# Reading the moving operand of a matmul alternately from two stretches: dense, block and value products of a two-layer hybrid encoder

## The chip, the cores and the metric

The kernel runs on one core of one Trainium2 chip. The metric is the device time of one execution in microseconds (us). Three runs of the kernel before the change took 1018.16, 1019.00 and 1019.24 us, a median of 1019.0 us. The profile shown here was taken from one further execution.

## The reference

The encoder has two layers on 512 tokens of 1024 features, in float32. Layer 0 mixes tokens with stick-breaking attention (16 heads of 64), layer 1 with a gated linear recurrence (RG-LRU); each is followed by an MLP with a squared ReLU. Cut to what matters:

```python
for layer in range(2):
    h = rms_norm(x, norm_mix[layer])
    if layer == 0:
        q, k, v = split(h @ w_qkv)               # 1024 -> 3 x 1024
        y = stick_breaking(q, k, v) @ w_o        # 1024 -> 1024
    else:
        proj = h @ w_in                          # 1024 -> 2 x 1024: gate, and input of the recurrence
        xc = causal_conv4(proj[:, 1024:])
        r, i = sigmoid(blocks(xc, w_a) + b_a), sigmoid(blocks(xc, w_x) + b_x)   # 16 blocks of 64 x 64
        y = (scan(r, i, xc) * gelu(proj[:, :1024])) @ w_ro
    x = x + y
    h = rms_norm(x, norm_mlp[layer])
    x = x + square(relu(h @ w1)) @ w2            # 1024 -> 4096 -> 1024
return rms_norm(x, norm_final)
```

## The kernel before

Activations lie with features on the 128 partitions and the 512 tokens along the free dimension (`x[c]`, c = 0..7). Every float32 product is made of three products of `float32r` halves: each operand is split into a high half (ScalarE, a `CAST`) and a low half (VectorE, a subtraction), and the matmuls high x high, low x high and high x low add up in one PSUM bank. So each of these products costs PE three matmuls, ACT one cast and DVE one subtraction of the weights (`wh`, `wl`).

There are four kinds of large products, named by the line of their matmul:

- **Dense**, L244 to L246 (`three`, called by `dense`, `beside` and the step generators): a 128x128 piece of a weight is stationary, and 512 tokens of one feature chunk (`xgh`, `xgl`, or `bh`, `bl`) stream past it. Query, key, attention output, the first quarter of each up-projection (`squared`), both halves of `w_in`, the output projection `w_ro`. L452 does the same for the first query and key; L1591 to L1593 for the gates of the recurrence.
- **Value**, L506 to L508 (`v_steps`): 128 tokens are stationary, and 256 columns of the value weight stream.
- **Block**, L1024 (`Mlp.up`): the other three quarters of the up-projection are done by a fast scheme with seven block products in place of eight; 256 tokens stream past a piece of 128 weight columns.
- **Down**, L1123 (`Mlp.times`): the down-projection in the same scheme. Activations are stationary, and 512 weight columns stream. These weights are stored on the host so that the program can read them alternately: the access pattern takes element 0 of the first 256 columns, then element 0 of the second 256, then element 1 of the first, and so on (`rearrange("p j (i n) -> p j n i", i=2)`), and the results land in PSUM in natural order. All other products read their moving operand straight through.

Scores (L590, L591) and the products of attention weights with values (L657, L658) are further matmuls, and L631 and L1406 are transposes on PE.

The order of the work on PE is the order in which the code calls it. Attention interleaves the fill (dense and value steps) with chains of scores and values by a table of due times (`SCORE0`, `VAL0`, `PACE`, in fill steps). The recurrence goes by the hand-written list `ORDER`, in which `P` is a dense product, `n` multiplies its PSUM bank by the norm factor (`scaled`), `b` and `t` are the convolution taps (`first_tap` on ACT, `taps` on DVE), `G` and `s` the gates and their sigmoids, and `z` the gate branch. In the MLP each step's weights are split some four steps ahead (`prepare`, `make`). On the other engines the steps of the recurrence and the MLP stand in the order of the code as well. There are eight PSUM banks, so a bank that is read late holds up the product that wants it next.

Consumers that read a PSUM bank of these products: `parted` and `k_halves` (query and key), `so_part`, `residual` (x plus product), `squared`, `leave` (the block products), `scaled`, `sigmoids`, `gate`.

Of the kernel before, what the change touches and what calls it, by code (L numbers as in the profile page):

```python
# [18 lines left out]
P = 128  # L19
# [48 lines left out]
def hybrid_encoder(  # L68
# [40 lines left out]
    def f(ap):  # L109
        return ap.bitcast(F32)  # L110

# [130 lines left out]
    def three(ps, ah, al, wh, wl, start, stop):  # L242

        PE.matmul(ps, wh, ah, start=start, stop=False)  # L244
        PE.matmul(ps, wl, ah, start=False, stop=False)  # L245
        PE.matmul(ps, wh, al, start=False, stop=stop)  # L246
# [68 lines left out]
    with ExitStack() as actx:  # L315
# [39 lines left out]
        def parted(x, tag):  # L355
# [3 lines left out]
            A.copy(xh, x)  # L359
            V.tensor_tensor(xl, x, f(xh), ALU.subtract)  # L360
            return xh, xl

        def q_halves(pair, ps):
            q[pair] = stacked("q", parted(ps, "x"))

        def first_halves(pq, pk):

            qh, ql = parted(pq, "x")
            h = hp.tile([P, S], F32R, tag="th", name="th", bufs=3)
            l = hp.tile([P, S], F32R, tag="tl", name="tl", bufs=3)  # L370
            A.copy(h, pk)
            V.tensor_tensor(l, pk, f(h), ALU.subtract)
# [9 lines left out]
        def k_halves(pair, ps):  # L382
            ks = hp.tile([P, S], F32, tag="ks", name="ks", bufs=1)
            V.tensor_tensor(ks, ps, norm["r"], ALU.mult)
            h, l = parted(ks, "x")
# [35 lines left out]
        with tc.manual_schedule(engines=others):  # L421
# [64 lines left out]
        def v_steps(m, tags=("acc",) * NB):  # L486
# [14 lines left out]
            for t in range(NB):  # L501
                ts = slice(t * P, (t + 1) * P)
                ps = bank(tags[t])[:, : 2 * P]
                for k in range(C):
                    wh, wl = (u[:, k % 4, :] for u in ws[k // 4])
                    PE.matmul(ps, xgh[:, k, ts], wh, start=k == 0, stop=False)  # L506
                    PE.matmul(ps, xgh[:, k, ts], wl, start=False, stop=False)
                    PE.matmul(ps, xgl[:, k, ts], wh, start=False, stop=k == C - 1)  # L508
# [12 lines left out]
        def so_part(c):  # L521
# [3 lines left out]
            for k in range(EARLY):  # L525
                three(ps, bh[:, k, :], bl[:, k, :], wh[:, k, :], wl[:, k, :], k == 0, k == EARLY - 1)
                if k == EARLY - 1:
                    early[c] = hp.tile([P, S], F32, tag="early", name="early")
                    A.copy(early[c], ps)
# [230 lines left out]
    def add_x(c, ps):  # L760
        V.tensor_tensor(x[c], x[c], ps, ALU.add)

    def residual(srcs, gname, begun={}, ready={}):

        for c in range(C):
            add_x(c, begun[c][0] if c in begun else dense(srcs[c], bh, bl, halves=ready.get(c)))
# [29 lines left out]
    class Mlp:  # L796
# [64 lines left out]
        def squared(self, c, also=None):  # L861
# [13 lines left out]
            self.A.activation(t, ps.rearrange("p (h n) -> p h n", h=2), AF.Relu)  # L875
# [139 lines left out]
        def up(self, name, w, ps, new):  # L1015
# [3 lines left out]
            for i in range(2):  # L1019
                for k in range(C // 2):  # L1020
                    h, l = self.xa(block, k)
                    wh, wl = (t[:, k, i * P : (i + 1) * P] for t in w)
                    for n, (m, y) in enumerate(((wh, h), (wl, h), (wh, l))):
                        PE.matmul(  # L1024
                            ps[:, i * HS : (i + 1) * HS], m, y,
# [134 lines left out]
        def run(self, first, between, end):  # L1160
# [89 lines left out]
            def leave(i):  # L1250
# [28 lines left out]
                u, three = us[p], bank.rearrange("p (i n) -> p i n", i=2)  # L1279
                keep = {"P1": 0, "P6": 1, "P5": 2, "P7": 3}.get(name)  # L1280
                if keep is not None:

                    self.A.copy(u[keep], three)
                at, x, y, op = {
                    "P3": (1, three, u[1], ALU.subtract),
                    "P7": (2, u[2], u[3], ALU.subtract),
                    "P2": (0, u[0], three, ALU.add),
                    "P4": (3, three, None, None),
                }.get(name, (None,) * 4)
                if op:  # L1290
                    self.V.tensor_tensor(u[at], x, y, op)
# [589 lines left out]
```

## Time and profile before

| | |
|---|---|
| median of three runs | 1019.0 us |
| the profiled execution | 1019.2 us |
| its span, first to last instruction | 1017.3 us |
| granted TensorE clock | 0.999 |
| idle time of ACT before its casts `wh<-b`, in all | 99.7 us |
| HBM read over the span | 139.51 MB |

A row of a timeline gives start, length, engine, line, operation, what it writes and reads, and the shape. Matmuls are pipelined: the length of one overlaps the next, so what a matmul costs PE is the distance from its start to the next one's start. A row of a stretch gives its length, and then per engine the busy time with the number of instructions in brackets.

### The profile page before, as it was taken

The numbers are of one execution on the slowest core, as the hardware profiler recorded it, in microseconds if no ns is written. First come the engines' busy times: TensorE is split into PE (matmuls) and PEld (weight loads), VectorE is DVE, ScalarE is ACT, GpSimd is POOL, SyncE is SP. The second block draws the span as 40 slices with busy tenths as digits, with TensorE's granted clock in tenths as the row PEclk, the third lists the DMA queues.
The fourth block names the chain that finished last, engine by engine and source line by source line (L and its number), as shares of the span: only waits on it lengthen the run. The fifth ranks groups of instructions, "written<-read, shape, count | busy, mean of one in ns | idle before, by whom it ended". The sixth has DMA issues, their size and how long they took to land.

```text
span 1017.3 us, 15902 instructions
## 1 busy us (share of the span) xinstructions
PE 1004.5 (99%) x5836; PEld 889.2 (87%) x5836; DVE 858.3 (84%) x1152; ACT 714.6 (70%) x1110; POOL 180.0 (18%) x243
## 2 busy tenths in 40 slices
PE   9999999999999999999999999999999999999997
PEld 7888888878888988998988888888889989989985
DVE  6878787857898799799799789985887799898898
ACT  6777676745778775774776699973887774874865
POOL 0454444430000110111011210300011110111112
PEclk9999999999999999999999999999999999999999
DMA  7845344536638667667783464445448977977953
GB/s 236 222 125 146 104 144 105 167 104 228 188 84 212 151 165 205 166 154 199 167 236 85 133 180 123 124 172 201 103 85 209 205 164 193 227 163 199 218 117 106
DMA packets 71901, 165.71 MB, mean 163 GB/s; under 512 B 23824, under 2 KB 25104, under 8 KB 71824
## 3 DMA queue, kind: packets, MB, share of 16 engines
q1 hardware_dynamic: 59424, 123.54, 38.4%
q0 software_dynamic: 11680, 40.38, 23.7%
q8 instruction: 46, 0.75, 0.3%
q10 hardware_dynamic: 720, 0.79, 0.2%
q14 instruction: 31, 0.25, 0.1%
HBM read 139.51 MB, written 6.29 MB: 143 GB/s over the span
## 4 chain that ended last, share of the span: by engine, by line
PE 65%; DVE 15%; ACT 11%; issue 5%; DMA 2%; POOL 0%; DVEq 0%; SPq 0%; ACTq 0%; POOLq 0%
PE ps_t L1123 9%; PE ps_acc L244 5%; PE ps_acc L246 5%; PE ps_acc L245 5%; PE ps_acc L1123 5%; PE ps_acc L1024 5%; ACT wh L786 4%; DVE wl L786 4%; DVE u L786 3%; ACT u L786 3%; PE ps_z L1123 3%; PE ps_t L244 2%; PE ps_t L245 2%; PE ps_t L246 2%; DVE b L786 2%
## 5 line engine op out<-in xcount | busy, mean ns | idle before, releaser
L786 ACT CAST wh<-b 128x1024 fp32r<-128x1024 f32 x168 | 173.8, 1047 | 99.7 <-DVE b L786 49.8
L786 DVE TENSOR_TENSOR wl<-b,wh 128x1024 fp32r<-128x1024 f32 x168 | 203.7, 1221 | 40.5 <-ACT wh L786 39.6
L1101 POOL DMA_DIRECT2D b<-in_w_dn x40 | 35.0, 876 | 347.7 <-DVE b L786 155.6
L244 PE MATMUL ps_acc<-xg,wh 128*128 128x512 f32 x200 | 81.7, 409 | 0.0
L1024 PE MATMUL ps_z<-xg,wh 128*128 128x256 f32 x384 | 78.9, 277 | 0.0
L246 PE MATMUL ps_acc<-xg,wh 128*128 128x512 f32 x200 | 78.5, 392 | 0.0
L245 PE MATMUL ps_acc<-xg,wl 128*128 128x512 f32 x200 | 78.4, 392 | 0.0
L239 DVE TENSOR_TENSOR wl<-raw,wh 128x512 fp32r<-128x512 f32 (+2 forms) x70 | 61.5, 905 | 14.5 <-ACT wh L237 14.3
L609 DVE TENSOR_TENSOR_SCAN scan<-keep,later 128x128 f32<-128x128 f32 (+1 forms) x64 | 58.8, 921 | 16.6 <-ACT keep L599 9.9
L786 ACT ACTIVATE u<-u 128x512 f32<-128x512 f32 x100 | 63.2, 632 | 11.1 <-DVE u L786 9.4
L237 ACT CAST wh<-raw 128x512 fp32r<-128x512 f32 (+2 forms) x70 | 50.6, 759 | 24.2 <-PE ps_acc L246 7.3
L1024 PE MATMUL ps_z<-xg,wl 128*128 128x256 f32 x240 | 66.4, 276 | 0.0
L1024 PEld LDWEIGHTS ps_z<-xg,wh 128*128 128x128 f32 x384 | 62.8, 188 | 0.2 <-ACT u L786 0.2
L1024 PE MATMUL ps_acc<-xg,wh 128*128 128x256 f32 x288 | 61.7, 278 | 0.0
L613 POOL TENSOR_TENSOR w<-w,scan 128x128 f32<-128x128 f32 (+1 forms) x64 | 51.4, 805 | 54.2 <-DVE scan L609 51.1
L786 DVE TENSOR_TENSOR b<-b,b 128x1024 f32<-128x1024 f32 x48 | 58.7, 1224 | 1.3
L786 DVE TENSOR_TENSOR u<-u 128x512 f32<-128x512 f32 (+1 forms) x92 | 54.8, 596 | 2.3 <-ACT u L786 1.1
L1101 POOL DMA_DIRECT2D b<-in_w_up x24 | 20.9, 869 | 197.3 <-DMA b<-in_w_up 84.4
L1024 PE MATMUL ps_acc<-xg,wl 128*128 128x256 f32 x192 | 53.2, 277 | 0.0
L1024 PE MATMUL ps_acc<-low,wh 128*128 128x256 f32 x192 | 53.2, 277 | 0.0
L786 ACT CAST wh<-raw 128x1024 fp32r<-128x1024 f32 x46 | 47.9, 1044 | 4.1 <-PE ps_acc L1123 4.0
L1123 PE MATMUL ps_t<-wh,sl 128*128 128x512 f32 x126 | 48.4, 384 | 0.8 <-DVE sl L786 0.6
(372 smaller groups left out, 3265.6 us busy)
## 6 DMA issues: line engine op xcount, KB each, us to landing
b<-in_w_dn SPq DMA_DIRECT2D x48, 512.0 KB, 4.9
b<-in_w_dn POOLq DMA_DIRECT2D x40, 512.0 KB, 5.6
b<-in_w_up SPq DMA_DIRECT2D x36, 512.0 KB, 4.6
b<-in_w_up POOLq DMA_DIRECT2D x24, 512.0 KB, 5.6
raw<-in_w_m SPq DMA_DIRECT2D x16, 512.0 KB, 4.6
raw<-in_w_dn SPq DMA_DIRECT2D x16, 512.0 KB, 4.7
raw<-in_w_in SPq DMA_DIRECT2D x16, 512.0 KB, 4.0
raw<-in_w_qk SPq DMA_DIRECT2D x12, 512.0 KB, 3.8
```

Source lines behind the costliest of these rows:

```text
L237: A.copy(wh[:, k, :], raw[:, k, :])
L239: V.tensor_tensor(wl[:, k, :], raw[:, k, :], f(wh[:, k, :]), ALU.subtract)
L244: PE.matmul(ps, wh, ah, start=start, stop=False)
L245: PE.matmul(ps, wl, ah, start=False, stop=False)
L246: PE.matmul(ps, wh, al, start=False, stop=stop)
L609: V.tensor_tensor_scan(sc[:, S - n : S][:, ::-1], keep[:, :n][:, ::-1], later[:, S - n :][:, ::-1], 1.0, ALU.mult, ALU.max,)
L613: G.tensor_tensor(wt, wt, sc[:, S - n + 1 : S + 1], ALU.mult)
L786: ins = getattr(self.e, name)(*args, **kwargs)
L1024: PE.matmul(ps[:, i * HS : (i + 1) * HS], m, y, start=new and i == k == n == 0, stop=i == 1 and k == C // 2 - 1 and n == 2, skip_group_che ...
L1101: G.dma_start(out=unit[b].rearrange("p j n -> p (j n)"), in_=unit["src"](to), accum_op=ALU.add)
L1123: PE.matmul(ps, m, y[:, jj], start=first and n == 0, stop=last and n == 2, skip_group_check=not new,)
```

## The change

The moving operand of the dense, value and block products is read alternately from the two halves of its columns, as the down product already does. `turns_of` makes the access pattern for the matmul's input; `as_read` views the output bank as pairs, so that PE still writes one PSUM element after the other. For activations the host can't reorder the columns, so the bank then holds token 0, token 256, token 1, token 257 and so on, and each consumer reads it with `in_order`, an access pattern with a step of two elements, and pairs it with a plain operand seen through `two`. For the value product the host reorders `w_v` instead. In a 512-column product the two stretches lie 256 elements apart, in a 256-column product 128.

One edit goes further: `scaled` no longer multiplies the bank in place. It writes the product, in natural order, to a tile `om[c]` in SBUF, which was allocated by `first_tap` before, and `first_tap` and `taps` read that tile.

```diff
+    def two(t):
+        return t.rearrange("p (i n) -> p i n", i=2)
+    def turns_of(t):
+        return t.rearrange("p (i n) -> p n i", i=2)
+    def as_read(ps):
+        return ps.rearrange("p (n i) -> p n i", i=2)
+    def in_order(ps):
+        return ps.rearrange("p (n i) -> p i n", i=2)
...
     def three(ps, ah, al, wh, wl, start, stop):
+        ps, ah, al = as_read(ps), turns_of(ah), turns_of(al)
         PE.matmul(ps, wh, ah, start=start, stop=False)
...
-            A.copy(xh, x)
-            V.tensor_tensor(xl, x, f(xh), ALU.subtract)
+            A.copy(two(xh), x)
+            V.tensor_tensor(two(xl), x, f(two(xh)), ALU.subtract)
...
-            V.tensor_tensor(ks, ps, norm["r"], ALU.mult)
+            V.tensor_tensor(two(ks), in_order(ps), two(norm["r"]), ALU.mult)
...
-                            first[i], parts[i][low][:, k, :], y[:, k, :], start=k == n == 0,
+                            as_read(first[i]), parts[i][low][:, k, :], turns_of(y[:, k, :]), start=k == n == 0,
...
-                    wh, wl = (u[:, k % 4, :] for u in ws[k // 4])
-                    PE.matmul(ps, xgh[:, k, ts], wh, start=k == 0, stop=False)
+                    wh, wl = (turns_of(u[:, k % 4, :]) for u in ws[k // 4])
+                    PE.matmul(to, xgh[:, k, ts], wh, start=k == 0, stop=False)
...
-    def add_x(c, ps):
-        V.tensor_tensor(x[c], x[c], ps, ALU.add)
...
+            ps = begun[c][0] if c in begun else dense(srcs[c], bh, bl, halves=ready.get(c))
+            V.tensor_tensor(two(x[c]), two(x[c]), in_order(ps), ALU.add)
...
-            self.A.activation(t, ps.rearrange("p (h n) -> p h n", h=2), AF.Relu)
+            self.A.activation(t, in_order(ps), AF.Relu)
...
-                            ps[:, i * HS : (i + 1) * HS], m, y,
+                            as_read(ps[:, i * HS : (i + 1) * HS]), m, turns_of(y),
...
-                u, three = us[p], bank.rearrange("p (i n) -> p i n", i=2)
+                u, three = us[p], bank.rearrange("p (i n h) -> p i h n", i=2, h=2)
...
         def scaled(c):
-            OV.tensor_tensor(ps[f"c{c}"], ps[f"c{c}"], r, ALU.mult)
+            om[c] = rp1.tile([P, S], F32, tag="om", name="om", bufs=C)
+            OV.tensor_tensor(two(om[c]), in_order(ps.pop(f"c{c}")), two(r), ALU.mult)
...
             OA.activation(
-                xc[c], ps[f"c{c}"], AF.Identity, bias=col("conv_b")[:, c : c + 1],
+                xc[c], om[c], AF.Identity, bias=col("conv_b")[:, c : c + 1],
...
-            x0, p = xc[c], ps.pop(f"c{c}")
+            x0, p = xc[c], om[c]
...
-                PE.matmul(pi, gh[:, i, :], xch, start=True, stop=False)
-                PE.matmul(pi, gl[:, i, :], xch, start=False, stop=False)
-                PE.matmul(pi, gh[:, i, :], xcl, start=False, stop=True)
+                three(pi, xch, xcl, gh[:, i, :], gl[:, i, :], True, True)
...
-                OA.activation(t[c], p, AF.Sigmoid, bias=col(b)[:, c : c + 1])
+                OA.activation(two(t[c]), in_order(p), AF.Sigmoid, bias=col(b)[:, c : c + 1])
...
-            OV.tensor_tensor(z[c], ps.pop(f"z{c}"), r, ALU.mult)
+            OV.tensor_tensor(two(z[c]), in_order(ps.pop(f"z{c}")), two(r), ALU.mult)
...
-            g["sb_w_qkv"][0][:, 2 * D :].reshape(2, 4, P, 4, 2 * P).transpose(3, 0, 2, 1, 4)
+            g["sb_w_qkv"][0][:, 2 * D :].reshape(2, 4, P, 4, P, 2).transpose(3, 0, 2, 1, 5, 4)
```

Each engine's instructions stand in the same order before and after, with the same operations and sizes; what differs is the lines' numbers, access patterns and, for the convolution, the tile that is read. The one place where the rows name another tile is the recurrence. On DVE, right after the reciprocal of the norm, the rows before are these (`ps_acc` and `ps_t` are PSUM banks, `bt` the convolution's output, `gl` the gates' low halves):

```order
L786 RECIPROCAL r<-r 128x512
L786 TENSOR_TENSOR ps_acc<-ps_acc,r 128x512 x2
L786 SCALAR_TENSOR_TENSOR bt<-ps_acc,colt,bt 128x511
L786 SCALAR_TENSOR_TENSOR bt<-ps_acc,colt,bt 128x510
L786 SCALAR_TENSOR_TENSOR bt<-ps_acc,colt,bt 128x509
L786 TENSOR_TENSOR ps_t<-ps_t,r 128x512
```

After the change the same place on DVE reads:

```order
L798 RECIPROCAL r<-r 128x512
L798 TENSOR_TENSOR om<-ps_acc,r 128x512 x2
L798 SCALAR_TENSOR_TENSOR bt<-om,colt,bt 128x511
L798 SCALAR_TENSOR_TENSOR bt<-om,colt,bt 128x510
L798 SCALAR_TENSOR_TENSOR bt<-om,colt,bt 128x509
L798 TENSOR_TENSOR om<-ps_t,r 128x512
```

Nothing moved in the order; the taps read SBUF in place of PSUM, and a bank's last reader is the multiplication instead of the third tap.

More of the change, by code (lines that the diff above doesn't have):

```diff
@@ L528, in so_part @@
                     early[c] = hp.tile([P, S], F32, tag="early", name="early")
-                    A.copy(early[c], ps)
+                    A.copy(two(early[c]), in_order(ps))
                 yield
@@ L1409, in feature @@
                 )
-            add_x(c, pt)
+            V.tensor_tensor(x[c], x[c], pt, ALU.add)
             last["low"] = halves("mix1", c, x[c])
```

37 lines of the change are left out of this document (19 added, 18 removed).

## The prediction

> **What bounds the kernel now.** I read the page first: the busy times (share of the span, count), then the chain of work that ended last.
>
> ```profile
> PE 1004.5 (99%) x5836; PEld 889.2 (87%) x5836; DVE 858.3 (84%) x1152; ACT 714.6 (70%) x1110; POOL 180.0 (18%) x243
> PE 65%; DVE 15%; ACT 11%; issue 5%; DMA 2%; POOL 0%; DVEq 0%; SPq 0%; ACTq 0%; POOLq 0%
> ```
>
> PE is hardly ever without a matmul, and two thirds of the chain are PE's. So the price of one matmul in a run is what matters, and then where DVE (84%) is close behind. The length of a matmul in the trace doesn't tell its price, because neighbours overlap; the distance between starts does. So next I read PE's timeline, the first and last row of runs without a wait (start, length, then the instruction): two runs of dense products, then a run of down products, which already read alternately.
>
> ```profile
> 17.55 0.39 PE L244 MATMUL ps_t<-xg,wh 128*128 128x512 f32 x1
> ...
> 22.15 0.39 PE L246 MATMUL ps_t<-xg,wh 128*128 128x512 f32 x1
> ...
> 700.51 0.39 PE L244 MATMUL ps_acc<-xg,wh 128*128 128x512 f32 x1
> ...
> 714.79 0.39 PE L244 MATMUL ps_z<-xg,wh 128*128 128x512 f32 x1
> ...
> 388.07 0.38 PE L1123 MATMUL ps_acc<-wh,bh 128*128 128x512 f32 x1
> ...
> 396.92 0.38 PE L1123 MATMUL ps_z<-wh,sl 128*128 128x512 f32 x1
> ```
>
> From the first to the last row are 20, 63 and 41 distances: 4.60/20 = **230 ns** for a dense matmul in attention, 14.28/63 = **226.7 ns** late in the program, 8.85/41 = **215.8 ns** for a down matmul. All have 512 columns, 128x128 weights and a new weight load each; the only difference that I see is how the moving operand is read. That is 14.2 or 10.9 ns a matmul. Now the same for 256 columns: block (straight), value (straight), and the few 256-column down products at the program's end (alternate).
>
> ```profile
> 417.81 0.28 PE L1024 MATMUL ps_acc<-low,wh 128*128 128x256 f32 x1
> ...
> 427.93 0.28 PE L1024 MATMUL ps_o<-s,wl 128*128 128x256 f32 x1
> ...
> 139.09 0.28 PE L506 MATMUL ps_acc<-wh,xg 128*128 128x256 f32 x1
> ...
> 141.09 0.28 PE L508 MATMUL ps_acc<-wh,xg 128*128 128x256 f32 x1
> ...
> 1007.74 0.27 PE L1123 MATMUL ps_o<-wh,bh 128*128 128x256 f32 x1
> ...
> 1010.31 0.28 PE L1123 MATMUL ps_o<-wh,sl 128*128 128x256 f32 x1
> ...
> 22.38 0.95 PE L462 MATMUL ps_z<-ones,ssq 128*128 128x1 f32 x8
> 23.19 0.48 PE L244 MATMUL ps_t<-xg,wh 128*128 128x512 f32 x1
> ```
>
> With 89, 17 and 23 distances: 10.12/89 = **113.7 ns**, 2.00/17 = **117.6 ns**, 2.57/23 = **111.7 ns**. The last pair says why the gap is small here: eight passes of a single column still take 0.81 us, 101 ns each, so with a new weight load for each a matmul can hardly go below that, however its columns are read.
>
> **The change part by part.** How many matmuls of each kind: these are the stretches of L244, in order (stretch, its length, PE busy with the count in brackets), then all of L1024 and of L506.
>
> ```profile
> 17.00:205.00 188.00, 53.46 (x126) 23.84 (x127) 1.00 0.53 144
> 205.00:245.00 40.00, 19.47 (x48) 9.02 (x48) 1.00 0.37 118
> 245.00:298.00 53.00, 25.97 (x67) 12.39 (x66) 1.00 0.58 185
> 550.00:572.00 22.00, 8.36 (x21) 4.14 (x22) 1.00 0.47 146
> 572.00:672.00 100.00, 50.82 (x130) 24.23 (x129) 1.00 0.47 121
> 672.00:701.00 29.00, 16.66 (x43) 7.93 (x43) 1.00 0.81 299
> 701.00:755.00 54.00, 24.64 (x63) 11.80 (x63) 1.00 0.31 78
> ...
> 0.00:1018.00 1018.00, 231.06 (x2016) 230.79 (x2016) 1.00 0.63 163
> ...
> 0.00:1018.00 1018.00, 36.69 (x128) 24.23 (x128) 1.00 0.63 163
> ```
>
> Each L244 stands for three matmuls (L244 to L246), each L506 for three (L506 to L508). The gates add 8 x 2 x 3 = 48 between 572 and 672, the first query and key (L452) 2 x 8 x 3 = 48 ahead of 17 us. PE's saving:
>
> - attention, dense: 3 x 126 = 378 x 14.2 ns = 5.4 us
> - the other dense ones and the gates: 3 x 372 + 48 = 1164 x 10.9 ns = 12.7 us (of it 572 to 672: 438, 4.8 us; the two stretches that end in an MLP: 201 and 189, 2.2 and 2.1 us)
> - first query and key: 48 x 10.9 ns = 0.5 us
> - value: 384 x 5.9 ns = 2.3 us
> - block: 2016 x 2.0 ns = 4.0 us
>
> Together **24.9 us**, if PE could use all of it. What lies behind PE decides the rest: busy times of PE, PEld, DVE, ACT and POOL (counts in brackets) in four stretches, and three timeline rows.
>
> ```profile
> 20.00:205.00 185.00, 184.58 (x1130) 162.74 (x1129) 152.35 (x244) 133.26 (x288) 77.17 (x121) 1.00 0.53 146
> 270.00:305.00 35.00, 34.21 (x157) 28.43 (x156) 32.99 (x61) 28.25 (x47) 3.15 (x4) 1.00 0.39 77
> 355.00:400.00 45.00, 44.63 (x258) 39.87 (x257) 43.98 (x51) 29.13 (x37) 4.35 (x5) 1.00 0.76 194
> 594.00:672.00 78.00, 78.00 (x345) 64.42 (x344) 71.21 (x101) 74.53 (x102) 15.68 (x13) 1.00 0.42 114
> ...
> 303.09 0.48 PE L1123 MATMUL ps_acc<-wl,sh 128*128 128x512 f32 x1 [0.62 <-DVE wl L786]
> ...
> 667.66 1.36 DVE L786 TENSOR_TENSOR bl<-z,bh 128x512 fp32r<-128x512 f32 x2 [0.26 <-ACT bh L786]
> 671.00 0.39 PE L246 MATMUL ps_o<-bl,wh 128*128 128x512 f32 x1
> ```
>
> - Attention (DVE 82%, ACT 72%): neither is full, both mostly wait for PE and come earlier with it. I take off 1.0 us of 7.7 for places where a chain is just in time.
> - Into each MLP (270 to 305: DVE 94%): PE already waits there for a low half of a weight (0.62 us at 303.09). What the dense products before it save in their second half turns into a longer wait: minus 1.1 us in each layer.
> - Block to down (355 to 400: DVE 98%): the second half of each block stretch hands its saving to DVE: minus 2.0 of 4.0 us.
> - Recurrence (594 to 672: ACT 96%): ACT hardly ever waits, so it won't come earlier by itself. PE can run ahead of it by the cover that it has. The first of the two `bl` at 667.66 is done 0.68 us later, at 668.3, and PE reads it at 671.00: 2.7 us of cover, plus what the stretch ahead of 594 gains. So some 3.4 of 4.8 us stay: minus 1.4 us.
> - First query and key: they wait for data as they arrive; minus 0.5 us.
>
> That leaves 24.9 - 7.1 = **17.8 us**. The profiled execution took 1019.2 us (span 1017.3 and 1.9 around it), 0.2 above the median of the runs: 1019.2 - 17.8 = 1001.4, so I say **1001 us**.
>
> The edits outside PE. `scaled` goes to SBUF and the taps read it there:
>
> ```profile
> L786 DVE TENSOR_TENSOR ps_acc<-ps_acc,r 128x512 f32<-128x512 f32 x5 | 3.4, 697 | 1.3 <-PE ps_acc L246 1.2
> L786 DVE TENSOR_TENSOR z<-ps_t,r 128x512 f32<-128x512 f32 x4 | 2.7, 682 | 0.0
> ...
> L786 DVE SCALAR_TENSOR_TENSOR bt<-ps_acc,colt,bt 128x510 f32<-128x510 f32 x5 | 3.7, 748 | 0.2
> L786 DVE SCALAR_TENSOR_TENSOR d<-a,om 128x512 f32<-128x512 f32 x8 | 5.5, 688 | 1.0 <-ACT om L786 1.0
> ```
>
> The same product costs 682 ns when its result goes to SBUF (697 in PSUM), and such an operation 688 ns with SBUF operands (748 from PSUM): up to 24 x 0.06 = 1.4 us less DVE work, which I count at nothing because ACT is the fuller one there. It adds no wait that isn't there by the data already: `om` has a buffer for each chunk, the sigmoid that overwrites it needs the taps' result anyway, and the bank comes free earlier.
>
> The unknown is a read of PSUM with a step of two elements; no row of before shows one. Its bounds are nothing, if these engines take an element a cycle wherever it lies, and twice the time for each element:
>
> ```profile
> L786 DVE TENSOR_TENSOR u<-u 128x512 f32<-128x512 f32 x60 | 41.3, 689 | 1.9 <-ACT u L786 1.1
> L786 DVE TENSOR_TENSOR u<-u 128x256 f32<-128x256 f32 x32 | 13.5, 423 | 0.4
> ...
> L786 ACT CAST s<-x 128x512 fp32r<-128x512 f32 x8 | 4.9, 616 | 0.0
> L786 ACT CAST s<-x 128x256 fp32r<-128x256 f32 x8 | 3.2, 402 | 0.0
> ```
>
> 256 elements more cost 266 ns on DVE and 214 on ACT, so doubling adds 0.53 and 0.43 us to each 512-column read. I take nothing: the operations are float32, one element at a time already (about 1 ns each), and the distance of the elements in a plain read gives them no advantage that these rows show. A read faster than now has no reason. In the code, DVE has 72 such reads and ACT 103.
>
> [...]
>
> **The rivals.**
>
> *All of it arrives.* The waits on DVE and ACT above may shrink, since both work partly on what PE hands them. Then all 24.9 us are saved: 994 us. For it: at 303.09 DVE's work was itself released by PE's earlier results. Against it: DVE's 94 to 98%.
>
> *The 256-column products gain nothing*, because the weight load is their floor (101 ns, and 113.7 is near it) or because two stretches 128 elements apart don't do what 256 apart do. Without the value's 2.3 and block's remaining 2.0 us: 1005.5 us.
>
> *The readers pay.* Doubled reads: 16 sigmoids add 16 x 0.43 = 6.9 us to an ACT that is full from 594 to 672, of which 2.7 are covered: 4.2 us later, and the 3.4 saved are gone. In each of the twelve block parts two DVE reads, every second part in the full stretch: 12 x 0.53 = 6.4 us. 17.8 - 3.4 - 4.2 - 6.4 = 3.8 us left: 1015 us.
>
> *Slower: short stretches collide.* In all 256-column products the stretches are only 128 elements (512 bytes) apart, and no row of before shows that; the alternate ones are 256 elements apart. If both stretches have to be fetched from the same place in turn, each column costs a fetch of its own. The 512-column products keep some 13.5 us, so from 13.5/2400 = 5.6 ns above today's 114 ns (about 119 ns) the kernel is slower; at double the columns' time, 2 x 111.7 = 223 ns, it is 2400 x 109 = 262 us less the 13.5, about 1268 us. For it: nothing in the trace but the lack of a row. Against it: 512 columns read alternately run at 215.8 with no loss, with DMAs at their busiest and at rest.
> [...]
>
> That the change doesn't do what it says (the program reading straight through after all) is excluded for 512 columns by the down product, where the same pattern stands in the code.
>
> **How the numbers follow.** Forecast (999 to 1004) 0.60; all of it arrives (992 to 998) 0.13; no gain at 256 columns (1004 to 1008) 0.12; the readers pay (1009 to 1016, or part of it) 0.08; collision (1020 and above) 0.07. The range of 992 to 1010 holds the first three and leaves 0.15 out. About 0.2% (2 us) is what a measurement of this kernel can tell from no change. Faster 0.91; within 0.2%, a nearly full doubling, 0.02; slower 0.07.
>
> **What would show it.** Right: dense matmuls some 216 ns apart in all stages, block and value 111 to 113; DVE's reads of `ps_` tiles as long as before (about 685 ns), ACT's too (575 to 690); longer waits on `wl` at the start of the down products and, from 594 to 672, on `bl` and `bh`. [...]

## The result, and the profile after

After the change the kernel takes **1002.36 us** (median of four runs, 1001.54 to 1003.18) against 1018.64 us for the kernel before in the same session (1018.16 to 1019.24). The ratio is 0.984, with a 95% interval of 0.9823 to 0.9857: 16.3 us, 1.6% faster. The profiled execution took 1003.18 us, its span 1001.3; the spans of the two profiled executions differ by 16.0 us. Two executions of the whole record took two to four times as long as their neighbours (2078 us of e5 and 3646 us of the kernel before beside e1, e2, e4 and e5) and count in no figure below.

The page of the kernel after, the same two lines as before the change: busy times of the engines, then the shares of the chain that ended last.

```profile
PE 983.0 (98%) x5836; PEld 884.0 (88%) x5836; DVE 858.0 (86%) x1152; ACT 715.4 (71%) x1110; POOL 176.4 (18%) x243
PE 39%; DVE 25%; ACT 22%; issue 8%; DMA 6%; SPq 0%; ACTq 0%; POOL 0%; DVEq 0%; POOLq 0%
```

PE has 21.5 us less busy time (1004.5 before), DVE and ACT as much as before. PE's share of the chain fell from 65% to 39%, DVE's rose from 15% to 25% and ACT's from 11% to 22%: the kernel now waits for the preparation of operands more often, and more of what PE is spared can be lost there.

PE's timeline of the kernel after, the first and last row of a run of dense products in attention, of block products and of value products (start, length, instruction):

```profile
18.68 0.38 PE L257 MATMUL ps_t<-xg,wh 128*128 128x512 f32 x1
...
23.00 0.38 PE L259 MATMUL ps_t<-xg,wh 128*128 128x512 f32 x1
...
409.60 0.28 PE L1036 MATMUL ps_acc<-low,wh 128*128 128x256 f32 x1
...
419.54 0.28 PE L1036 MATMUL ps_o<-s,wl 128*128 128x256 f32 x1
...
136.53 0.27 PE L520 MATMUL ps_acc<-wh,xg 128*128 128x256 f32 x1
...
138.43 0.28 PE L522 MATMUL ps_acc<-wh,xg 128*128 128x256 f32 x1
```

20, 89 and 17 distances lie between: 4.32/20 = 216 ns, 9.94/89 = 111.7 ns and 1.90/17 = 111.8 ns. They are the same runs that the prediction measured at 230, 113.7 and 117.6 ns. A dense matmul costs 215.8 ns in every stage now. What made it dearer in attention (230 ns) than late in the program (226.7) in the kernel before, no run shows.

The readers of these banks, groups of DVE and ACT (busy us, mean ns of one, idle time before): first three of the kernel before, then the same and the taps of the kernel after.

```profile
L761 DVE TENSOR_TENSOR x<-x,ps_acc 128x512 f32<-128x512 f32 x4 | 2.7, 688 | 3.5 <-PE ps_acc L246 3.5
L786 ACT COPY u<-ps_z 128x512 f32<-128x512 f32 x18 | 10.5, 581 | 2.7 <-PE ps_z L1024 2.7
L786 ACT ACTIVATE aa<-ps_o,colt 128x512 f32<-128x512 f32 x4 | 2.8, 689 | 1.8 <-PE ps_o L1593 1.8
```

```profile
L778 DVE TENSOR_TENSOR x<-x,ps_acc 128x512 f32<-128x512 f32 x4 | 2.7, 687 | 3.2 <-PE ps_acc L259 3.2
L798 ACT COPY u<-ps_z 128x512 f32<-128x512 f32 x18 | 10.5, 582 | 1.3 <-PE ps_z L1036 1.3
L798 ACT ACTIVATE aa<-ps_o,colt 128x512 f32<-128x512 f32 x4 | 2.7, 687 | 0.4 <-PE ps_o L259 0.4
L798 DVE TENSOR_TENSOR om<-ps_acc,r 128x512 f32<-128x512 f32 x5 | 3.3, 681 | 0.1
L798 DVE SCALAR_TENSOR_TENSOR bt<-om,colt,bt 128x510 f32<-128x510 f32 x8 | 6.0, 750 | 0.3
```

A read of PSUM with a step of two elements costs what a plain one did: 688 and 687, 581 and 582, 689 and 687 ns. The scaling fell from 697 to 681 ns as its result went to SBUF; the taps did not get cheaper there (748 ns from PSUM, 750 from SBUF). The prediction's bound of 688 ns was an operation that multiplies by a constant (`d<-a,om`), while the taps multiply by a column with one value for each partition (`colt`). A row of before with such a column, and all its operands in SBUF, was as dear as the taps:

```profile
L155 DVE SCALAR_TENSOR_TENSOR xg<-x,colt,xg 128x512 fp32r<-128x512 f32 x32 | 23.8, 763 | 4.7 <-ACT xg L154 4.7
```

Where the 16.0 us are: the two traces have the same 5836 matmuls in the same order, so the start of one and the same matmul can be looked up in both, and the difference grows by what was saved in between. In us, beside the terms of the prediction (saved on PE, and less what it took off):

| from, to (time before) | work | saved on PE by the prediction | expected to stay | measured |
|---|---|---|---|---|
| 0 to 17.5 | first query and key | 0.5 | 0 | -1.1 |
| 17.5 to 205 | attention: dense, value | 7.7 | 6.7 | 6.3 |
| 205 to 306 | dense, and into MLP 0 | 3.8 | 2.7 | 2.8 |
| 306 to 550, 755 to the end | block and down | 4.0 | 2.0 | 0.85 |
| 550 to 672 | dense and gates, recurrence | 5.5 | 4.1 | 3.8 |
| 672 to 755 | dense, and into MLP 1 | 3.5 | 2.4 | 3.4 |
| sum (the prediction's 24.9 and 17.8, rounded by stretch) | | 25.0 | 17.9 | 16.05 |

The stretch of 306 to 550 is read off these rows of PE's timeline, before and then after:

```profile
306.00 0.38 PE L1123 MATMUL ps_t<-wh,bl 128*128 128x512 f32 x1
...
550.06 0.38 PE L1123 MATMUL ps_t<-wh,bl 128*128 128x512 f32 x1
```

```profile
297.96 0.38 PE L1135 MATMUL ps_t<-wh,bl 128*128 128x512 f32 x1
...
541.70 0.38 PE L1135 MATMUL ps_t<-wh,bl 128*128 128x512 f32 x1
```

244.06 us before, 243.74 after: three quarters of the MLP with 1008 block products saved 0.3 us. The first row of the table is arrival of data at the program's start (ACT's first operations on `x` wait 3.0 us for the DMA in after, 2.1 in before) and differs from run to run: in e1 below, whose code there is that of after, the same point comes 0.36 us earlier than before, not 1.1 later.

The first rows are also less sure than the last ones. The attention stretch takes 181.3 us in after and 181.2, 182.0, 182.0 and 183.1 in e3, e5, e11 and e12, where its work is the same; it takes 187.6 in before and 187.0 in e2 and e4. A late start is partly made up there: counted from the first matmul, the first two rows together last 198.8 to 199.2 us in after, e5, e11 and e12 (196.8 in e3), though the first alone lasts 15.8 to 17.6. So these two rows are better read as one: 5.2 us saved, where 6.7 were expected. The stretch from 205 to 306 takes 97.8 to 98.0 in after, e3 and e12, but 100.9 in e5 and 102.6 in e11, where PE stood once or twice for some us. The stretches from 550 to 672 and from 672 to 755 agree to 0.4 and 0.5 us among these traces.

Where the block's saving went stands in the view of what PE waited for (us in total, times, longest), before and after:

```profile
PE ps_acc L1123 <- DVE wl L786: 1.4, 3, 0.6
PE ps_t L1123 <- DVE sl L786: 0.6, 2, 0.3
PE ps_z L1123 <- DVE wl L786: 0.2, 1, 0.2
```

```profile
PE ps_t L1135 <- DVE sl L798: 1.9, 6, 0.3
PE ps_acc L1135 <- DVE wl L798: 1.4, 3, 0.6
PE ps_z L1036 <- ACT u L798: 1.0, 3, 0.6
PE ps_z L1135 <- DVE wl L798: 1.0, 1, 1.0
```

The down products now wait longer for low halves that DVE makes (`sl` 0.6 to 1.9, `wl` in `ps_z` 0.2 to 1.0), and the block products wait 1.0 us for ACT's copies of banks, which was no row before. All distances from the start of a block product to the next matmul add up to 230.1 us before and 227.3 after, those of the down products to 298.2 and 301.2: what the block gives, the down takes.

Four stretches of the kernel after, in its own time, so that they hold somewhat later work than the same stretches of before (busy us of PE, PEld, DVE, ACT, POOL):

```profile
20.00:205.00 185.00, 183.37 (x1160) 166.50 (x1159) 157.50 (x253) 138.07 (x298) 81.68 (x127) 1.00 0.57 152
270.00:305.00 35.00, 33.38 (x156) 28.39 (x156) 33.90 (x77) 30.14 (x48) 3.48 (x4) 1.00 0.55 112
355.00:400.00 45.00, 44.60 (x240) 39.11 (x239) 42.85 (x50) 26.38 (x33) 5.72 (x7) 1.00 0.72 177
594.00:672.00 78.00, 77.45 (x355) 66.36 (x354) 71.57 (x101) 71.12 (x98) 9.86 (x11) 1.00 0.45 126
```

Into the first MLP (270 to 305) DVE is busy 33.90 of 35 us and PE 33.38: there PE is no longer the fullest engine (262 to 297, some 8 us earlier and so nearer to the work that the kernel before does from 270 to 305, shows 33.99 and 33.38).

### The profile page after: what moved, and what is told of

Same layout as the page of the kernel before. It is cut to its first block, busy times and chain, and to the rows that moved or that the text cites. A ratio compares the mean times of both kernels' runs of the same rounds, so it can differ in the third digit from the quotient of the medians.

```text
span 1001.3 us, 15918 instructions
## 1 busy us (share of the span) xinstructions
PE 983.0 (98%) x5836; PEld 884.0 (88%) x5836; DVE 858.0 (86%) x1152; ACT 715.4 (71%) x1110; POOL 176.4 (18%) x243
## 4 chain that ended last, share of the span: by engine, by line
PE 39%; DVE 25%; ACT 22%; issue 8%; DMA 6%; SPq 0%; ACTq 0%; POOL 0%; DVEq 0%; POOLq 0%
PE ps_t L1135 8%; DVE wl L798 6%; ACT wh L798 6%; PE ps_acc L1135 4%; DVE u L798 4%; ACT u L798 3%; PE ps_acc L1036 3%; DVE b L798 3%; PE ps_acc L257 3%; PE ps_acc L259 3%; PE ps_acc L258 2%; PE ps_z L1135 2%; ACT bh L798 2%; DVE c L798 2%; ACT L798 2%
## 5 line engine op out<-in xcount | busy, mean ns | idle before, releaser
L257 PE MATMUL ps_acc<-xg,wh 128*128 128x512 f32 x200 | 79.1, 395 | 0.0
L259 PE MATMUL ps_acc<-xg,wh 128*128 128x512 f32 x200 | 75.8, 379 | 0.0
L258 PE MATMUL ps_acc<-xg,wl 128*128 128x512 f32 x200 | 75.8, 379 | 0.0
L623 DVE TENSOR_TENSOR_SCAN scan<-keep,later 128x128 f32<-128x128 f32 (+1 forms) x64 | 59.3, 929 | 12.9 <-ACT keep L613 6.5
L1113 POOL DMA_DIRECT2D b<-in_w_up x24 | 20.9, 869 | 196.8 <-DMA b<-in_w_up 84.4
```

The costliest lines, as they stand in the source:

```text
L623: V.tensor_tensor_scan(sc[:, S - n : S][:, ::-1], keep[:, :n][:, ::-1], later[:, S - n :][:, ::-1], 1.0, ALU.mult, ALU.max,)
L1113: G.dma_start(out=unit[b].rearrange("p j n -> p (j n)"), in_=unit["src"](to), accum_op=ALU.add)
```

## Experiments

The theory was: (1) a matmul's price depends on how its moving operand is read, and two stretches in turn are the cheap way; (2) the readers pay nothing; (3) what doesn't arrive is lost to DVE, in the MLP above all. Rivals: the block part gains nothing or everything; the loss lies elsewhere; it is the new way of reading in itself, or the distance between the stretches, that matters. Twelve kernels ran.

**e1 and e2: the parts apart.** e1 is the kernel after with block and value products read straight again; e2 is the kernel before with the block products alone read alternately (and their readers in order).

```diff
 e1, from after
-                            as_read(ps[:, i * HS : (i + 1) * HS]), m, turns_of(y),
+                            ps[:, i * HS : (i + 1) * HS], m, y,
...
-                    wh, wl = (turns_of(u[:, k % 4, :]) for u in ws[k // 4])
+                    wh, wl = (u[:, k % 4, :] for u in ws[k // 4])
...
```

> The changed kernel with the block and value products read straight again (dense ones, the gates and the first query and key stay alternate). Theory A: the block products' saving ends in waits on DVE (the trace of the changed kernel keeps 0.85 us of it over all block and down stretches) and the value products bring some 2.0 us, so this takes 1002.4 + 2.9 = 1005.3 us. Rival B: the block products bring what the spacing of their matmuls says, 2016 x 2.0 ns = 4.0 us, and more is lost elsewhere: 1008.5 us. Dense matmuls stay 216 ns apart, block ones go back to 113.7.

> The kernel before with the block products alone read alternately. Theory A: 1018.6 - 0.9 = 1017.7 us, with block matmuls 111.7 ns apart and longer waits on low halves at the start of the down products. Rival B: 1018.6 - 4.0 = 1014.6 us.

e1: 1006.37 us (1004.61 to 1006.68), ratio 0.9865 [0.985, 0.9879]; e2: 1018.23 us beside 1019.25 for the kernel before, ratio 0.9986 [0.9978, 0.9995]. Each beside the kernel before of its own session, the dense part alone brings some 12.9 us, block and value together 3.4 more (16.3 for the whole; 2.7 between the spans of the two traces), and the block alone 1.0. e2 lies by its theory A (1017.7) and far from its rival of 1014.6; e1 lies between its two. In e2 the block products are at 111.7 ns, the first and last of 335 distances being these rows of its timeline (37.41/335):

```profile
403.77 0.27 PE L1024 MATMUL ps_acc<-xg,wh 128*128 128x256 f32 x1
...
441.18 0.28 PE L1024 MATMUL ps_z<-xg,wh 128*128 128x256 f32 x1
```

Their distances add up to 227.1 us (230.1 before), those of the down products to 300.1 (298.2 before): 3.0 saved, 1.9 given back in the next stage, with no other part of the change in the kernel. The traces of e6, e7, e10 and e11, whose block and down products are those of after, show the same: 226.9 to 227.3 and 300.1 to 300.2. The block's part of the gain is between 0.85 us (by stretch, after) and 1.8 (by stretch, after against e1), where the prediction had 2.0.

**e3: the other direction.** The down products, which read alternately in both kernels, are read straight, and the host stores their weights in natural order.

```diff
...
-                t.rearrange("p j (i n) -> p j n i", i=2)[:, :, cols.start // 2 : cols.stop // 2, :]
-                for t in w
...
+            wh, wl = (t[:, :, cols] for t in w)
...
```

> The changed kernel with the down products read straight (their weights stored in natural order on the host). Theory A, the read of the moving operand is what costs the 11 ns: down matmuls go from 216 to about 227 ns at the very same place; PE needs 1332 x 11 = 14.7 us more, of which up to 6 us come out of waits on DVE: 1011 to 1017 us. Rival B, the spacing belongs to the place (its weight loads, its neighbours): down matmuls stay at 216 ns and the time at 1002.4 us.

1011.8 us (1010.76 to 1011.99), ratio 0.993 [0.9913, 0.9947]: some 9 us slower than after. A run of 129 down products in its timeline:

```profile
367.38 0.39 PE L1131 MATMUL ps_z<-wh,bl 128*128 128x512 f32 x1
...
396.65 0.39 PE L1131 MATMUL ps_t<-wh,sl 128*128 128x512 f32 x1
```

29.27/129 = 226.9 ns, where the same run takes 215.8 in after. So the 11 ns belong to the way of reading and not to the kind of product. 1332 x 11 ns are 14.7 us; some 9 to 10 arrive, because the waits in the down products shrink at the same time (the distances above the usual one add up to 6.3 us, 11.0 in after). These waits work both ways: what PE spends there is partly paid with them.

**e4 and e5: relieving DVE.** Both leave out the 48 additions of two weight blocks (`b<-b,b`, 1.22 us each) that DVE makes for the fast scheme, e4 from the kernel before, e5 from the kernel after; the weights of those products are then not the scheme's.

```diff
-            elif to:
-                self.V.tensor_tensor(unit[b], unit[b], unit[to], ALU.add)
```

> The kernel before without the 48 additions of two weight blocks on DVE (1.22 us each, 58.7 us of DVE work); the weights of some block and down products are then not the sums that the scheme needs. It is the base for the next run. With DVE relieved the PE waits in block and down stretches go: 1013 to 1017 us in all theories.

> The changed kernel without the same 48 additions on DVE. Theory A, DVE takes the block products' saving: with DVE relieved it arrives, and this is 19 to 20.5 us faster than the run before without additions (16.3 us with them). Rival B, something else takes it (ACT, DMA, the weight loads): the distance stays at 16 to 17 us.

e4 takes 1016.28 us (1014.36 to 1020.74), ratio 0.9969 [0.9956, 0.9982]; e5 995.63 (the median of 994.55, 995.63 and 997.71), ratio 0.9758 [0.9738, 0.9777]. Without the additions the change brings some 20.7 us in place of 16.3. By stretch, block and down together save 3.4 us between 306 and 550 and 4.1 after 755, 7.5 in all, where they save 0.85 with the additions in place. The distances of the block products add up to 234.7 us in e4 and 227.1 in e5, those of the down products to 290.6 and 290.8: nothing is given back. The waits of PE in block and down products, in e4 and then in e5:

```profile
PE ps_acc L1024 <- ACT u L786: 2.5, 1, 2.5
...
PE ps_z L1121 <- DVE wl L786: 0.2, 1, 0.2
```

```profile
PE ps_acc L1036 <- ACT u L798: 1.7, 1, 1.7
...
PE ps_z L1133 <- DVE wl L798: 0.2, 1, 0.2
```

This shows that the block's saving is lost by way of these additions: without them the waits of the down products for DVE are all but gone, and the saving stays. Whether it is DVE's time or the weights' wait for the sum that counts is not told apart here. Nor does the pair show the 4.0 us arriving as they were, because the straight block products were dearer in e4 (234.7 us) than in the kernel before (230.1): 2.5 us of that is the one wait for ACT, and the rest is their price, on average 115.0 ns without waits where before had 114.0. Why that price moves stays open.

**e6, e7, e10 and e11: what about the reading is cheap.** In these four the dense products alone read in other orders (`three`); the consumers still read the bank as two stretches, so tokens are out of order in the output. e6 reads the even tokens and then the odd ones, in one stretch with a step of two; e7 takes 32 stretches of 16 elements in turn, neighbours 64 bytes apart; e10 4, 8 or 16 stretches, from product to product; e11 always two in turn, at four distances. The view of the output bank is changed along with the read, so that PE writes one PSUM element after the other as before; that line is left out below.

```diff
-        ps, ah, al = as_read(ps), turns_of(ah), turns_of(al)
 e6
+        ah, al = (t.rearrange("p (n i) -> p i n", i=2) for t in (ah, al))
 e7
+        ah, al = (t.rearrange("p (i n) -> p n i", i=32) for t in (ah, al))
 e10
+        i = (4, 8, 16)[turn[0] % 3]
+        ah, al = (t.rearrange("p (i n) -> p n i", i=i) for t in (ah, al))
 e11
+        n = (128, 64, 32, 16)[turn[0] % 4]
+        ah, al = (t.rearrange("p (b i n) -> p b n i", i=2, n=n) for t in (ah, al))
```

> The changed kernel with the dense products (512 columns) read first at all even, then at all odd elements, a single stretch with a step of two elements; the consumers are left as they are, so tokens come out in another order than the reference's. Theory A, the straight read is slow because neighbours lie next to each other, and two places in turn help: a single stretch with a step gives no help, 227 ns or more a matmul, 1016 us or more. Rival B, any pattern that isn't a plain run of elements is as quick: 216 ns, 1002 us.

> The changed kernel with the dense products read from 32 stretches of 16 elements in turn (neighbouring reads 64 bytes apart instead of 1024); consumers as they are, so tokens come out in another order. Theory A, any two places in turn will do: 216 ns and 1002 us. Rival C, they must be far apart (the block products' 512 bytes were enough): above 227 ns, and each ns above 216 costs 1.5 us: 1018 us and more.

> After, with the dense products taking in turn 4 stretches of 128 elements (neighbours 512 bytes apart), 8 of 64 (256 bytes) and 16 of 32 (128 bytes); the consumers still read the bank as two stretches, so tokens are out of order in the output. Theory A (two reads that lie in one short piece of memory collide, and the piece is 64 bytes or a little more): all three at 216 ns, about 1002 us. Rival B (the collision grows as the distance falls): 216 at 512 bytes and between 220 and 435 at 256 or 128. Rival C (more than two stretches are what doubles it, not the distance): all three at some 433 ns, about 1330 us.

> After, with each dense product reading always two stretches in turn, as after, but in four distances, one product after the other: 128, 64, 32 or 16 elements (512, 256, 128, 64 bytes); a stretch that is through is followed by the next pair. The consumers still read the bank as two stretches, so tokens are out of order in the output. Theory A (the distance decides): 64 and 128 bytes at some 433 ns, 256 at some 487 or less, 512 between 216 and 283, as in the two runs with many stretches. Rival B (the number of stretches in turn decides, two are free at any distance): all four at 216 ns, about 1002 us in all. Rival C (the collision needs both: many stretches and a short distance): 64 bytes above 216, the others at 216.

The programs took 1358.4, 1329.0, 1287.7 and 1007.5 us, the last two in a single execution each. First and last row of a run of dense products in the timelines of e6 (724 distances), e7 (724), e10 (23 distances with 8 stretches in turn, then 44 with 4) and e11 (278, in which all four distances occur):

```profile
745.23 0.65 PE L259 MATMUL ps_t<-xg,wl 128*128 128x512 f32 x1
...
1072.36 0.63 PE L260 MATMUL ps_t<-xg,wh 128*128 128x512 f32 x1
```

```profile
730.44 0.62 PE L259 MATMUL ps_t<-xg,wl 128*128 128x512 f32 x1
...
1044.19 0.61 PE L260 MATMUL ps_t<-xg,wh 128*128 128x512 f32 x1
```

```profile
902.09 0.69 PE L262 MATMUL ps_o<-bh,wh 128*128 128x512 f32 x1
...
913.28 0.69 PE L264 MATMUL ps_o<-bl,wh 128*128 128x512 f32 x1
...
342.02 0.46 PE L262 MATMUL ps_o<-xg,wh 128*128 128x512 f32 x1
...
354.48 0.45 PE L264 MATMUL ps_o<-xg,wh 128*128 128x512 f32 x1
```

```profile
588.30 0.38 PE L262 MATMUL ps_o<-bh,gh 128*128 128x512 f32 x1
...
648.30 0.38 PE L264 MATMUL ps_t<-xg,wh 128*128 128x512 f32 x1
```

| order of reading, 512 columns | ns a matmul |
|---|---|
| straight (before) | 226.7 to 230 |
| two stretches in turn, 1024, 512, 256, 128 or 64 bytes apart (after, e11) | 215.8 |
| 4 in turn, neighbours 512 bytes apart (e10) | 283 |
| 8 in turn, 256 bytes (e10) | 487 |
| 16 in turn, 128 bytes (e10) | 434 |
| 32 in turn, 64 bytes (e7) | 433 |
| one stretch, step of two elements (e6) | 452 |

e6 lies above theory A's bound of 227 ns, but not as meant: I had expected the straight price, and it doubled. e7 was first read as a collision of addresses 64 bytes apart. e10 took that away, since 4 stretches 512 bytes apart cost more than two (none of its three expectations came true), and e11 shows, as its rival B had it, that with two in turn any of the four distances is free. So distance alone doesn't cost. That the number alone does is not shown: with four and more, number and distance changed together, eight cost more than sixteen, and a single stretch with a step of two is among the dearest. What makes these patterns dear is open. e11's dense matmuls cost 215.8 ns at all four distances; its 5.1 us above after are mostly one wait of PE, 3.9 us at 244.7 us, for an addition to `x` on DVE.

**e8 and e9: going further.** e8 turns the scores as well, and the products of attention weights with values, for which the halves of the weights are written to SBUF alternately. e9 turns the scores alone.

```diff
 e8 and e9
+                    to = as_read(z[:, :nn])
+                    PE.matmul(to, lhsT, turns_of(kh[pair][j][:, :nn]), start=True, stop=False)
...
 e8 alone
-                    dh, dl, q0 = th[:, :n], tl[:, :n], kb * P
+                    dh, dl, q0 = turns_of(th[:, :n]), turns_of(tl[:, :n]), kb * P
...
```

> The changed kernel with the scores and the products of attention weights with values read alternately too: the readers of the scores take them in order from PSUM, and the high and low halves of the turned attention weights are written to SBUF in the order in which the alternate read brings them back natural. Theory A: 32 matmuls of 512, 384 and 64 of 256 columns in each of the two save 17, 12 and 6 ns, 2.6 us of PE in all; attention's other engines are 75 to 85% busy and some 70% arrive: 1000.5 us, never slower than 1002.4. Rival B: writing the halves alternately to SBUF costs ACT and DVE time on the chain from transposes to products, which was just in time: 1003 us or more.

> After, with the scores' matmuls too reading their moving operand (the key halves, 128 to 512 columns) alternately, and the sigmoids and the multiplication behind them reading the bank back in order; the attention weights are written and read straight. Theory A (the price of a matmul falls with the way its moving operand is read, and it is the alternate writes to SBUF, not the alternate reads, that cost the run with scores and weights turned its gain): the scores come to some 216 and 111 ns as in that run, ACT's and DVE's rows on the transposed weights stay at 588 and 678 ns, PE needs some 1.3 us less, of which 0.5 to 1.1 arrive: 1001.3 to 1002. Theory B (attention's end is set by ACT and DVE, PE's saving there turns into waits): within 0.3 us of after, 1002.1 to 1002.7. Rival C (the alternate reads of the scores' banks are what cost that run its gain): 1004 or more, with sigmoids longer than 700 ns.

e8: 1005.08 us (1004.74 to 1007.72), ratio 0.9869 [0.9854, 0.9884], 2.7 us slower than after (2.1, each beside the kernel before of its session). Its matmuls did get cheaper (the scores' and weights' with 256 columns have medians of 110 to 112 ns, 117 to 119 before), but two groups nearly doubled; these are the rows of e8, below them that of e9 for the first and that of after for the second:

```profile
L664 ACT CAST th<-ps_t 128x512 fp32r<-128x512 f32 x16 | 17.5, 1091 | 5.9 <-PE ps_t L648 5.8
L665 DVE TENSOR_TENSOR tl<-ps_t,th 128x512 fp32r<-128x512 f32 x16 | 18.0, 1123 | 11.6 <-ACT th L664 11.6
```

```profile
L663 ACT CAST th<-ps_t 128x512 fp32r<-128x512 f32 x16 | 9.4, 588 | 6.1 <-PE ps_t L648 6.1
```

```profile
L661 DVE TENSOR_TENSOR tl<-ps_t,th 128x512 fp32r<-128x512 f32 x16 | 10.8, 678 | 8.9 <-ACT th L660 8.9
```

A write to SBUF that jumps between two stretches costs ACT 1091 ns in place of 588. DVE's operation takes 1123 ns in place of 678; it also reads `th` from SBUF in the same jumping order, so its write alone is not shown. e9 has no such accesses on these engines and shows the readers of the scores' banks as they were (ACT's sigmoids of 512 columns 700 and 694 ns, in after 696 and 689), but it wins nothing: 1003.57 us (1003.05 to 1006.38), ratio 0.9856 [0.9837, 0.9875], not to be told from after's 0.984, and above the ranges of its theories A and B. PE needs 1.5 us less between 20 and 205 us (181.82 for 183.37), and a matmul at 205 us starts at the same time in both traces to within 0.1 us, although e9's first dense product started 1.0 us earlier. So this saving didn't arrive in these two traces; as traces of the same code differ by up to 2 us in attention, 1.5 us is near what they can tell.

**e12: moving work from DVE to POOL.** e4 and e5 point to a faster kernel: the additions of one product (`P6`) go to POOL, which is busy 18% of the span.

```diff
-                self.V.tensor_tensor(unit[b], unit[b], unit[to], ALU.add)
+                (G if name == "P6" else self.V).tensor_tensor(unit[b], unit[b], unit[to], ALU.add)
```

> After, with the addition of the sixth product's weights (b11 plus b22, 128x1024, in the block stretches and the down stretches) on POOL in place of DVE, in the same place of the order. Theory A (in these stretches it is DVE's fill, 218 of 244 us, that turns PE's saving into waits of the down products): some 20 additions of 1.22 us leave DVE, at least 25 us, the waits of the down products fall from 11.0 to below 7 us, 997 to 1000.5 us. Rival B (POOL takes 2 us or more for one, and the weights' halves that wait for it come later than from DVE): the waits stay at 10 us or more, 1002 or more. Rival C (POOL and DVE hinder each other): as B, with DVE's 128x1024 subtractions longer than 1.22 us.

1018.09 us, ratio 0.9978 [0.9968, 0.9988]: nearly all of the change's gain is lost. Groups of POOL and ACT and a row of PE's waits in e12, then DVE's row of these additions in after:

```profile
L1117 POOL TENSOR_TENSOR b<-b,b 128x1024 f32<-128x1024 f32 x20 | 54.7, 2734 | 42.5 <-DVE wl L798 42.5
L798 ACT CAST wh<-b 128x1024 fp32r<-128x1024 f32 x168 | 173.4, 1048 | 118.7 <-POOL b L1117 59.7 <-DVE b L798 25.1 <-PE ps_t L1135 15.1
PE ps_z L1036 <- ACT u L798: 9.5, 12, 2.3
```

```profile
L798 DVE TENSOR_TENSOR b<-b,b 128x1024 f32<-128x1024 f32 x48 | 58.7, 1223 | 1.3
```

One addition takes POOL 2.73 us, DVE 1.22. ACT, which makes the high half of the sum next, stands 59.7 us behind POOL, and its copies of the block products' banks stand behind that cast in its queue; so PE waits 9.5 us for them (1.0 in after). DVE's 128x1024 subtractions stay at 1.22 us, as in after; its 21 subtractions `sl<-u,sh` (128x512) between 306 and 550 us rise from 684 to 810 ns on average. What lengthens these no run shows, nor whether DVE slows POOL. DVE did have 29 us less work between 306 and 550 and 755 and 1000 (408.9 for 437.9; the twenty additions are 24.5 of it), and it didn't help: the later sums cost more than the relief brought. How much of that is the longer addition, and how much POOL's own wait for DVE ahead of it (42.5 us of its idle time), is not told apart. Of e4 and e5 it therefore stays open how much of their gain is DVE's time and how much is that the weights no longer wait for a sum.

## Why the prediction was right, and where it was off

The prediction was 1001 us in a range of 992 to 1010; 1002.4 came. It forecast 17.8 us less for the profiled execution, and 16.0 came. Part of that closeness is luck: by the table, attention with the program's start brought 1.5 us less than expected and block and down 1.2 less, and the second MLP brought 1.0 more.

- **The price of a matmul by its way of reading: right.** 215.8 ns in all stages and 111.7 ns at 256 columns were taken from the down product's rows, and both came out to the tenth. e3 shows it from the other side: the same down products, read straight, cost 226.9.
- **256 columns gain 2.0 and 5.9 ns: right.** The rival "no gain at 256 columns" falls by the block products' 111.7 ns in e2, where nothing else was changed. That a new weight load sets a floor near 101 ns there was my estimate from the row of eight single-column passes; no run varied the weight loads.
- **Readers pay nothing: right**, by the rows of 687, 582 and 687 ns above. That these engines take one element at a time was my estimate from the 266 and 214 ns for 256 elements more. The argument that the distance of the elements doesn't matter holds for these reads of PSUM; it does not hold for ACT's write to SBUF that jumps between two stretches (1091 ns for 588 in e8).
- **The taps: off, and counted at nothing.** I had bounded them by an operation with SBUF operands and a constant factor (688 ns); they stayed at 750, near the 763 of the row of before with a column as factor.
- **Attention, minus 1.0, and the first query and key, minus 0.5: too small together.** By its own row attention saved 6.3 of 7.7, where 6.7 were expected, but with the start it is 5.2. Traces of the same work leave 3.9 to 6.4 us for attention alone. Which chain holds it up no run isolates; in e9 a further 1.5 us did not arrive.
- **Recurrence, minus 1.4: about right in sum.** 3.8 of 5.5 arrived between 550 and 672, 4.1 were expected. The loss lies where it was put: in after the starts of matmuls on `bh` and `bl` between 644 and 660 us lie up to 650 ns apart. That ACT's fill and PE's cover set its size was only argued; no run changed them.
- **Into each MLP, minus 1.1: right for the first, wrong for the second.** The first lost what was expected (2.8 stayed of 3.8). In the second 3.4 of 3.5 arrived: I had taken the wait seen at 303.09 us for both layers, without a row of the second.
- **Block to down, minus 2.0 of 4.0: right in kind, too small in size.** 0.85 us arrived by stretch and not 2.0 (1.8 against e1, 1.0 in e2). I had assumed that only the second half of each block stretch hands its saving on. In the trace of after the down products take 3.0 us more and the block products wait 1.0 us for ACT; e2 gives back 1.9 of 3.0 with nothing else changed, and in e5, without the additions, none is given back. That it is DVE's fill that takes it, as the prediction says, is not shown apart from the weights' wait for the sums (e12).
- **Collision: no at two stretches, yes beyond.** The rival that would have made it slower was 512-byte neighbours in 256 columns. They cost nothing (111.7 ns), nor do 64 bytes in 512 columns (215.8 ns, e11). The price I had given it, double, is about what 8 or more stretches in turn (433 to 487 ns) and a step of two elements (452 ns) do cost.

## What to carry to other kernels

Measure the price of a matmul as the distance between starts, for each way in which its moving operand is read, and if one kind of product in the same trace is cheaper, that row is the forecast for the others; two stretches in turn with PSUM written in order (215.8 ns for 226.7 to 230), and readers that put it back in order (687 ns for 688 on DVE, 582 for 581 on ACT), cost nothing elsewhere here, but more stretches in turn made the matmuls dearer (283 to 487 ns), and a write to SBUF that jumps between two stretches nearly doubled ACT's operation (1091 ns for 588). Then ask for each stage which engine hands PE its operands, since a stage's saving can be lost in the next one: a saving of 3 us on the block products left 1. Before moving work off a full engine, ask whether the other engine delivers it as early (2.73 us for an addition on POOL, 1.22 on DVE), and what stands behind the waiting instruction in its queue (9.5 us of PE's waits in e12, 1.0 in after).

## What the hardware showed that was not expected

- A straight read isn't the fastest read of a float32r moving operand: 226.7 to 230 ns for 512 columns against 215.8 for two stretches in turn. The straight price also varies (unbroken runs of 70 to 335 distances of block products in the kernel before have means of 113.5 to 116.4 ns), the alternate one hardly (111.7 to 111.8 in after).
- Four stretches in turn cost 283 ns, eight 487, sixteen and thirty-two 433 to 434, and a step of two elements in one stretch 452.
- A read of PSUM with a step of two elements costs DVE and ACT nothing (687 ns for 688, 582 for 581). A write to SBUF that jumps between two stretches costs ACT 1091 ns for 588; DVE, which reads one SBUF operand in that order as well, 1123 for 678.
- A multiply-add on DVE with a factor for each partition takes as long with its operands in SBUF (750 and 763 ns) as from PSUM (748); with a constant factor 688 were seen.
- POOL takes 2.73 us for a 128x1024 addition that takes DVE 1.22.
